# Three pairs of neighbouring RWKV stages become one stage each

## The chip, the cores and the metric

The kernel runs on one core of one Trainium2 chip. The core has a matrix engine (TensorE, called PE in the profile, with PEld for its weight loads), a vector engine (VectorE, DVE), an activation engine (ScalarE, ACT), GpSimd (POOL) and SyncE (SP), which issues most of the DMAs. The metric is the time of one execution on the device in microseconds, the median over several runs.

## The reference

One decoder block over 256 tokens plus 16 meta tokens, width 2048: a norm, one wide projection `w_in`, two token mixers in parallel, a gated merge, the output projection, and a SwiGLU feed-forward. The mixers are RWKV-7 (16 heads of 64) and FoX, a softmax attention with a forget gate (16 heads of 64). The part that this change touches is RWKV's recurrence over time,

```python
def step(S, inp):
    r_t, w_t, k_t, v_t, a_t, b_t = inp
    sa = jnp.einsum('bhvk,bhk->bhv', S, a_t)
    S = (S * w_t[:, :, None, :] + sa[..., None] * b_t[:, :, None, :]
         + v_t[..., None] * k_t[:, :, None, :])
    return S, jnp.einsum('bhvk,bhk->bhv', S, r_t)
```

followed by a group norm per head, a bonus term and a gate. Everything is float32.

## The kernel before

Weights stream from HBM in blocks of 128 x 1024. Each is split into a rounded high part and a rest (`wh` on ACT, L321; `wl` on DVE, L322), and the products high x high, high x low and low x high are summed in PSUM by the faster float32 mode of PE. L351 to L353 are these matmuls with three instructions for each weight tile (`f`, `k`, `v`, `r`), L427 and L429 the form with two (`zg`, `gt`, `up` and FoX's q). Buffers for the split weights are four deep.

RWKV and FoX are worked in four groups of four heads each. For group g the order of the weight jobs is k, v, r, the small LoRA products, FoX's q, k, v, and then two gate jobs (`zg`); for g = 3 the remaining gate jobs follow. The recurrence is cut into chunks of 64 tokens, with the meta tokens as a chunk of 16 ahead, so that most of it becomes small matmuls. All this small work of a group is a Python generator, `rwkv_bg` (from L724), which yields at the end of every stage the time after which its next stage is due; `fox_bg` is the same for FoX, and `head_norms` serves both.

The planner that interleaves them is `slot` (L383): PE's order is written out by hand, and after each pair of weight tile and k index (a slot: 340 ns of planner time for 272 columns, 322.5 for 258, 320 for 256) it looks for the stream that has been due the longest, runs one stage of it, and then lets none run until the larger of GAP = 250 ns and MIX = 0.47 times the PE time that the stage counted. Planner time is a plain sum of slots; it does not contain the stages' own time. `pe_mm` counts 4 x columns / 2.4 ns for a call, `pe_tr` 128 / 2.4 ns. A FoX stage that needs PE's aux buffers waits up to HOLD = 3500 ns for a stage of the RWKV chain, so that both run as one. Only PE's order is fixed so; the order on DVE, ACT and POOL is made by the compiler's scheduler out of the program's dependences.

A call of `pe_mm` in full float32 leaves two records in the trace, a transpose one.

The stages of `rwkv_bg` around the change, in order, each with what it needs of the aux pool (four PSUM buffers, 8 - PSM):

| stage | lines | PE work, calls | aux buffers | read out by | yields (ns) |
|---|---|---|---|---|---|
| mat, m = 0 | 790 to 798 | 8 matmuls, 64 rows, both heads of a pair side by side | 2 | DVE, 128x512 each (L796) | 2900 |
| mat, m = 1 | the same | 8 more | 2 | DVE | 2900 |
| mat0 | 799 to 829 | 4 matmuls of 80 columns for the meta chunk | 2 | DVE (L805); then DMAs L814, L816, L820 and POOL copies L823, L827 | 2300 |
| bonus (bs) | 831 to 839 | 4 matmuls against a block of ones | 2 | DVE (L837) | 1200 |
| trbk, m = 0 | 846 to 852 | 4 transposes | 1 | ACT (L850) | 1400 |
| trbk, m = 1 | the same | 4 | 1 | ACT | 1400 |
| trv | 853 to 861 | 4 transposes | 1 | ACT (L859) | 1100 |
| tr0 | 862 to 870 | 4 transposes (`tr` in the trace) | 1 | ACT (L866, L868) | 1600 |
| lane solve | 872 to 893 | none; 31 steps of two operations on DVE (L881, L883) on the table `ln` | | | 1000 after each fourth step, 24000 at its end |
| chain | 895 on | rhs, u, QT, X, s, y, ... | 1 or 2 | ACT, DVE | |

The table `ln` of the lane solve is gathered from the mat blocks NK through DRAM: NK to `d1` (L814 and L816), `d1` to `ln` (L820). Its result goes back the same way (L887, L891, L892) and is first used by the chain. The other stages that matter near these are FoX's k norms (`fk`: L644 to L648, two aux buffers, four matmuls in two pairs, each pair into one buffer), FoX's value transposes (`pvm`, `pv`: L1082 to L1088, two buffers), and the previous group's `yT` (four transposes, one buffer).

Of the kernel before, what the change touches and what calls it, by code (L numbers as in the profile page):

```python
# [62 lines left out]

HOP = 3050
PREP = 5200
LANE = 24000
GAP = 250

HOLD = 3500
# [17 lines left out]
Y_MAT = 2900  # L87
Y_NEXT = 2300
Y_BONUS = 1200
Y_TRBK = 1400  # L90
Y_TRV = 1100
Y_TR0 = 1600
Y_RHS = 1400
Y_U = 1400
Y_XT = 1400
# [7 lines left out]
def hybrid_block(ctx, tc, A, out, dbg=None):  # L103
# [18 lines left out]
    def aux_ps(name):  # L122
        return psa.tile([P, 512], F32, tag="aux", name=name)
# [251 lines left out]
    def pe_mm(out_, lhsT, rhs, start, stop, skip=False):  # L375
        clock[2] += 4 * max(lhsT.shape[-1], rhs.free_size()) / 2.4
        nc.tensor.matmul(out_, lhsT, rhs, start=start, stop=stop, skip_group_check=skip)

    def pe_tr(out_, in_, ident_):
        clock[2] += P / 2.4  # L380
        nc.tensor.transpose(out_, in_, ident_)
# [284 lines left out]
    def rwkv_jobs(g):  # L666
# [24 lines left out]
        def mul(w):  # L691
            (uh, ul), (gh, gl) = w
            gg = box["gg"] = ot(f"gg{g}")
            for m in range(2):
                ms = slice(m * P, (m + 1) * P)
                ps = main_ps(f"g{g}{m}")[:, :T]
                for k in range(2):
                    mm3(ps, gh[:, k, ms], gl[:, k, ms], sgh[:, k, :], sgl[:, k, :], k == 0, k == 1)
                nc.vector.tensor_copy(gg[:, m, :], ps)
            with tc.manual_schedule(engines={nc.scalar.engine}):  # L700
                for nm, i, dh, dl, bname in (("sig", 0, twh, twl, "w0"), ("aa", 1, adh, adl, "a0")):
                    dst = box[nm] = et(f"{nm}{g}")
                    for m in range(2):
                        ms = slice(m * P, (m + 1) * P)
                        ps = (aux_ps if i == 0 else main_ps)(f"{nm}{g}{m}")[:, :L]
                        mm3(ps, uh[:, i, ms], ul[:, i, ms], dh, dl, True, True)
                        nc.scalar.activation(dst[:, m, :], ps, AF.Sigmoid, bias=vc(bname, 2 * g + m))

                nc.scalar.preload_act_table_set("natural_log_exp_and_others")
            spawn(rwkv_bg(g, box), HOP)  # L710
# [3 lines left out]
    def hb(h):  # L714
        return slice(h * HD, (h + 1) * HD)

    def tok(c):

        return slice(0, HD) if c < 0 else slice(NMETA + c * HD, NMETA + (c + 1) * HD)

    def bcast(ap, n):
        return ap.unsqueeze(1).to_broadcast([P, n, ap.shape[1]])

    def rwkv_bg(g, box):  # L724
# [64 lines left out]
        for m in range(2):  # L789
            pss = [aux_ps(f"mat{g}{m}{h}") for h in range(2)]  # L790
            for c in range(4):
                for h in range(2):
                    pe_mm(pss[h][:, c * P:(c + 1) * P], bk[hb(h), m, c].rearrange("p x t -> p (x t)"),
                                     ar[hb(h), :, m, tok(c)], start=True, stop=True)
            for h in range(2):
                nc.vector.tensor_tensor(NK[:, h, 4 * m:4 * m + 4, :], pss[h].rearrange("p (c w) -> p c w", w=P),  # L796
                                        bcast(mup, 4), op=ALU.mult)
            yield Y_MAT
        pss = [aux_ps(f"mat0{g}{h}") for h in range(2)]
        for m in range(2):  # L800
            for h in range(2):
# [44 lines left out]
        for m in range(2):  # L846
            ps = aux_ps(f"trbk{g}{m}")
            for c in range(4):
                pe_tr(ps[:, c * P:(c + 1) * P], bkf[:, 4 * m + c, :], ident)
            nc.scalar.activation(BK[:, :, 4 * m:4 * m + 4, :].rearrange("p h c d -> p c h d"),  # L850
                                 ps.rearrange("p (c h d) -> p c h d", h=2, d=HD), AF.Copy)
            yield Y_TRBK
        ps = aux_ps(f"trv{g}")
        for m in range(2):
            for e in range(2):
# [2 lines left out]
        for cc in range(2):  # L858
            nc.scalar.activation(SV[HD:, :, cc::2, :].rearrange("p h i d -> p i h d"),  # L859
                                 ps[hb(cc), :].rearrange("p (i h d) -> p i h d", h=2, d=HD), AF.Copy)  # L860
        yield Y_TRV
        ps = aux_ps(f"tr0{g}")
        for m in range(2):
            pe_tr(ps[:, m * P:(m + 1) * P], bk0[:, m].rearrange("p x t -> p (x t)"), ident)
# [4 lines left out]
                             ps[:NMETA, 2 * P:].rearrange("p (m h d) -> p m h d", h=2, d=HD), AF.Copy)  # L869
        yield Y_TR0  # L870

# [17 lines left out]
        for h in range(2):  # L889
            for q in range(2):  # L890
                nc.sync.dma_start(X[h * HD + 32 * q:h * HD + 32 * q + 32, :, 32 * q:32 * q + 32], d2v[h, q, :32])  # L891
            nc.sync.dma_start(X0[h * HD:h * HD + 16, :, 0:32], d2[32:, :16].rearrange("(h m) r t -> h r m t", h=2)[h])  # L892
        yield LANE, ("chain", 1)

# [554 lines left out]
```

## Time and profile before

| | us |
|---|---|
| median of three runs | 1534.19 |
| lowest, highest | 1533.04, 1534.68 |
| the profiled execution's own time | 1533.9 |
| its span, first to last instruction | 1532.2 |
| PE busy | 1525.6 |
| DVE busy | 1031.3 |
| ACT busy | 778.7 |

The four groups of RWKV and FoX lie within about the first 590 us; after them come the merge and the feed-forward, which the change does not touch. Times in the timeline are microseconds from the span's start: start, duration, engine, line, operation, output <- inputs, shape, count. An `x16` row is a run of sixteen records. A row's bracket gives the idle time of the engine before it and what ended it.

### The profile page before, as it was taken

Reading aid. Unit: us, or ns where it says so; the run is one execution under the profiler, and the core shown is the slowest. Engines: PE = TensorE matmul, PEld = TensorE weight load, DVE = VectorE, ACT = ScalarE, POOL = GpSimd, SP = SyncE. Lnnn points to the kernel's source line nnn. Section 1 sums busy time; section 2 is a strip of 40 time slices with the busy share of each in tenths; the row PEclk is TensorE's granted clock in tenths of the full one; section 3 lists DMA queues with packets and bytes.
Section 4 is the critical chain, followed back from the end, with each engine's and each line's share of the span. In section 5 each row is a group of like instructions: output and inputs, shape, how many; then the busy total and the mean of one; then the engine's idle time right before and its main releaser. Section 6 shows DMA issues by size and latency. Waiting matters only on the chain.

```text
span 1532.2 us, 25930 instructions
## 1 busy us (share of the span) xinstructions
PE 1525.6 (100%) x10113; PEld 1348.9 (88%) x10113; DVE 1031.3 (67%) x1859; ACT 778.7 (51%) x1176; POOL 102.6 (7%) x182
## 2 busy tenths in 40 slices
PE   9999999999999999999999999999999999999998
PEld 9999999999989888998888888888888888888887
DVE  7888698689689768776566566656556665444443
ACT  7654665565475545554455455545445554333332
POOL 2111202302202100000000000000000000000000
PEclk9999999999999999999999999999999999999999
DMA  8667456646646757767566666666666666666663
GB/s 270 172 173 195 130 144 191 170 125 170 184 125 168 215 140 232 234 218 236 186 182 182 191 186 187 191 187 186 190 189 185 189 192 186 189 203 206 188 203 104
DMA packets 211643, 283.30 MB, mean 185 GB/s; under 512 B 24064, under 2 KB 128528, under 8 KB 211520
## 3 DMA queue, kind: packets, MB, share of 16 engines
q1 hardware_dynamic: 206912, 277.51, 61.8%
q10 hardware_dynamic: 4608, 4.13, 0.8%
q8 instruction: 79, 1.29, 0.4%
q14 instruction: 44, 0.36, 0.1%
HBM read 274.36 MB, written 7.24 MB: 184 GB/s over the span
## 4 chain that ended last, share of the span: by engine, by line
PE 99%; DMA 0%; DVE 0%; ACT 0%; SPq 0%; issue 0%; ACTq 0%
PE up L427 11%; PE gt L427 10%; PE zg L427 8%; PE dn L1312 5%; PE dn L1311 5%; PE dn L1310 5%; PE up L429 5%; PE gt L429 5%; PE zg L429 4%; PE f L351 2%; PE f L353 2%; PE f L352 2%; PE f L427 2%; PE br L351 2%; PE br L352 2%; PE br L353 2%
## 5 line engine op out<-in xcount | busy, mean ns | idle before, releaser
L322 DVE TENSOR_TENSOR wl<-raw,wh 128x1024 fp32r<-128x1024 f32 x488 | 598.8, 1228 | 414.2 <-ACT wh L321 413.7
L321 ACT ACTIVATE wh<-raw 128x1024 fp32r<-128x1024 f32 x488 | 515.9, 1058 | 605.6 <-PE dn L1311 141.5
L427 PE MATMUL gt<-hts,wh 128*128 128x512 f32 x704 | 245.0, 394 | 0.0
L427 PE MATMUL up<-hts,wh 128*128 128x512 f32 x704 | 244.9, 394 | 0.0
L429 PE MATMUL gt<-hts,wl 128*128 128x256 f32 x660 | 186.2, 282 | 0.0
L429 PE MATMUL up<-hts,wl 128*128 128x256 f32 x660 | 186.0, 282 | 0.0
L427 PE MATMUL zg<-xhl,wh 128*128 128x512 f32 x512 | 182.4, 401 | 0.0
L427 PEld LDWEIGHTS up<-hts,wh 128*128 128x128 f32 x704 | 130.1, 188 | 26.4
L427 PEld LDWEIGHTS gt<-hts,wh 128*128 128x128 f32 x704 | 130.1, 188 | 26.3
L1311 PE MATMUL dn<-wh,acl 128*128 128x512 f32 x352 | 138.7, 394 | 0.0
L1312 PE MATMUL dn<-wl,ach 128*128 128x512 f32 x352 | 138.3, 393 | 0.0
L1310 PE MATMUL dn<-wh,ach 128*128 128x512 f32 x352 | 138.1, 392 | 0.0
L429 PE MATMUL zg<-xhl,wl 128*128 128x256 f32 x480 | 135.0, 281 | 0.0
L429 PEld LDWEIGHTS up<-hts,wl 128*128 128x128 f32 x660 | 124.7, 189 | 1.8
L429 PEld LDWEIGHTS gt<-hts,wl 128*128 128x128 f32 x660 | 124.7, 189 | 1.8
L427 PEld LDWEIGHTS zg<-xhl,wh 128*128 128x128 f32 x512 | 94.3, 188 | 19.4 <-issue 0.7
L429 PEld LDWEIGHTS zg<-xhl,wl 128*128 128x128 f32 x480 | 90.6, 189 | 1.2
L1310 PEld LDWEIGHTS dn<-wh,ach 128*128 128x128 f32 x352 | 66.0, 188 | 15.7
L1311 PEld LDWEIGHTS dn<-wh,acl 128*128 128x128 f32 x352 | 66.1, 188 | 15.4
L1312 PEld LDWEIGHTS dn<-wl,ach 128*128 128x128 f32 x352 | 66.1, 188 | 14.7
L351 PE MATMUL f<-xhl,wh 128*128 128x272 f32 x256 | 76.3, 298 | 0.0
L353 PE MATMUL f<-xhl,wl 128*128 128x272 f32 x256 | 73.7, 288 | 0.0
(463 smaller groups left out, 2787.6 us busy)
## 6 DMA issues: line engine op xcount, KB each, us to landing
raw<-in_w_gate_up_dram SPq DMA_DIRECT2D x176, 512.0 KB, 4.4
raw<-in_w_in_dram SPq DMA_DIRECT2D x160, 512.0 KB, 3.9
raw<-in_w_down_dram SPq DMA_DIRECT2D x88, 512.0 KB, 4.7
raw<-in_w_o_dram SPq DMA_DIRECT2D x32, 512.0 KB, 3.9
raw<-in_w_branch_a_dram SPq DMA_DIRECT2D x16, 512.0 KB, 4.6
raw<-in_w_branch_b_dram SPq DMA_DIRECT2D x16, 512.0 KB, 3.7
zgd<-zg ACTq DMA_DIRECT2D x30, 128.0 KB, 3.8
gate<-zgd SPq DMA_DIRECT2D x15, 256.0 KB, 4.6
```

What stands on the lines that cost most here:

```text
L321: nc.scalar.activation(th, rr, AF.Copy)
L322: nc.vector.tensor_tensor(tl, rr, th.bitcast(F32), op=ALU.subtract)
L351: nc.tensor.matmul(ps, wh, ah, start=first, stop=False)
L352: nc.tensor.matmul(ps, wh, al, start=False, stop=False)
L353: nc.tensor.matmul(ps, wl, ah, start=False, stop=last)
L427: nc.tensor.matmul(ps.rearrange("p (a t) -> p a t", a=2), wh, act, start=first, stop=last)
L429: nc.tensor.matmul(ps[:, :T], wl, act[:, 0, :], start=False, stop=False)
L1310: nc.tensor.matmul(o, ah[:, kt, ts_], hi, start=first, stop=False)
L1311: nc.tensor.matmul(o, al[:, kt, ts_], hi, start=False, stop=False)
L1312: nc.tensor.matmul(o, ah[:, kt, ts_], lo_, start=False, stop=last)
```

## The change

The second mat block no longer yields, so mat0 runs in the same stage. The two trbk blocks become one stage, and trv and tr0 one. The distances that fell away are added to others: `Y_TRBK` is 2800 in place of twice 1400, `Y_TR0` 2700 in place of 1100 and 1600, and the 2900 that stood between mat and mat0 go to `LANE`, the distance between the end of the lane solve and the chain.

```diff
-LANE = 24000
+LANE = 26900
-Y_TRBK = 1400
-Y_TRV = 1100
-Y_TR0 = 1600
+Y_TRBK = 2800
+Y_TR0 = 2700
@@ rwkv_bg, mat
                 nc.vector.tensor_tensor(NK[:, h, 4 * m:4 * m + 4, :], pss[h].rearrange("p (c w) -> p c w", w=P),
                                         bcast(mup, 4), op=ALU.mult)
-            yield Y_MAT
+            if m == 0:
+                yield Y_MAT
@@ rwkv_bg, trbk
             nc.scalar.activation(BK[:, :, 4 * m:4 * m + 4, :].rearrange("p h c d -> p c h d"),
                                  ps.rearrange("p (c h d) -> p c h d", h=2, d=HD), AF.Copy)
-            yield Y_TRBK
+        yield Y_TRBK
@@ rwkv_bg, trv
             nc.scalar.activation(SV[HD:, :, cc::2, :].rearrange("p h i d -> p i h d"),
                                  ps[hb(cc), :].rearrange("p (i h d) -> p i h d", h=2, d=HD), AF.Copy)
-        yield Y_TRV
         ps = aux_ps(f"tr0{g}")
```

## The prediction

> **What bounds the kernel now.** I read the page first: span, busy shares, granted clock and the chain of work that ended last.
>
> ```profile
> span 1532.2 us, 25930 instructions
> PE   1525.6 (100%) x10113; PEld 1348.9 (88%) x10113; DVE 1031.3 (67%) x1859; ACT 778.7 (51%) x1176; POOL 102.6 (7%) x182
> PEclk9999999999999999999999999999999999999999
> PE 99%; DMA 0%; DVE 0%; ACT 0%; SPq 0%; issue 0%; ACTq 0%
> ```
>
> TensorE (PE) is busy for all but 6.6 us of the span, at full clock, and 99% of the chain is PE. So only two things can move the time: the length of the PE instruction stream, or a new moment in which PE stands still. DVE, ACT, POOL and the queues count only through such a moment. A busy PE hides short stalls, so I read start times in the timeline instead of busy time: in the stream of weight matmuls a start follows the last at a fixed pitch, and what a stage inserts is the stretch of starts less that pitch. The columns are start, duration, engine, line, operation.
>
> **The mat stages (group 2), each with the weight matmuls around it.**
>
> ```profile
> 343.98 0.29 PE L353 MATMUL f<-xhl,wl 128*128 128x272 f32 x1
> 344.20 1.16 PE L377 MATMUL mat<-ar,bk 64*128 64x128 f32 x16
> ...
> 345.52 0.29 PE L352 MATMUL f<-xhl,wh 128*128 128x272 f32 x1
> ...
> 346.52 0.29 PE L647 MATMUL fk<-nhfk,bones 128*128 128x272 f32 x1
> ...
> 346.77 0.29 PE L647 MATMUL fk<-nhfk,bones 128*128 128x272 f32 x1
> ...
> 349.13 0.29 PE L353 MATMUL f<-xhl,wl 128*128 128x272 f32 x1
> 349.35 0.46 PE L377 MATMUL mat<-ar,bk 64*80 64x16 f32 x8
> ...
> 349.98 0.29 PE L352 MATMUL f<-xhl,wh 128*128 128x272 f32 x1
> ```
>
> The two fk starts are two pitches apart: 346.77 - 346.52 = 0.25 us. From the weight matmul ahead of the second mat stage to the second one behind it, 345.52 - 343.98 = 1.54 us; less two pitches the stage costs 1.29 us. The mat0 stage costs 349.98 - 349.13 - 0.25 = 0.60 us.
>
> What of this is the price of coming and going? The trace has the same kind of small stage alone and in company:
>
> ```profile
> 330.44 0.29 PE L353 MATMUL f<-xhl,wl 128*128 128x272 f32 x1
> 330.65 0.45 PE L377 MATMUL u<-R,X 64*64 64x64 f32 x8
> 330.93 0.40 PE L377 MATMUL y<-S,ar 64*64 64x64 f32 x8
> ...
> 331.50 0.29 PE L352 MATMUL f<-xhl,wh 128*128 128x272 f32 x1
> ...
> 333.12 0.29 PE L353 MATMUL f<-xhl,wl 128*128 128x272 f32 x1
> 333.34 0.45 PE L377 MATMUL y<-sv,NK 128*64 128x64 f32 x8
> ...
> 333.95 0.29 PE L352 MATMUL f<-xhl,wh 128*128 128x272 f32 x1
> ```
>
> Sixteen records in one stage cost 331.50 - 330.44 - 0.25 = 0.81 us, eight alone 333.95 - 333.12 - 0.25 = 0.58 us. Eight more in company therefore cost 0.23, and a stage of its own costs 0.35 us for the change of form there and back. Putting mat0 behind the second mat block removes one such change. Its bounds are 0 (the change from 128 to 80 columns costs as much as the change to the weight matmuls) and 0.35 (as u and y). I take 0.30, nearer to u and y, because both blocks keep the same two 64-row halves; 0.05 is left for the odd column count. Four groups: **-1.2 us**, bounds -1.4 and 0.
>
> The rows show that a change of tile form costs PE time. The Trainium skill, TensorEngine Tiling (Array Packing), section Key Properties, says the same in general: changing the tiling mode drains the engine; by that rule too the pair mat and mat0 would save one drain and the sum stays.
>
> **The transposes.** Here the same reading gives another answer:
>
> ```profile
> 111.42 0.28 PE L429 MATMUL zg<-xhl,wl 128*128 128x256 f32 x1
> 111.54 0.60 PE L381 MATMUL trbk<-ident,bk 128*128 128x128 f32 x4
> ...
> 112.21 0.28 PE L429 MATMUL zg<-xhl,wl 128*128 128x256 f32 x1
> ...
> 237.06 0.28 PE L429 MATMUL zg<-xhl,wl 128*128 128x256 f32 x1
> 237.18 0.27 PE L381 MATMUL pvm<-ident,vv 128*16 128x128 f32 x1
> ...
> 238.07 0.28 PE L429 MATMUL zg<-xhl,wl 128*128 128x256 f32 x1
> ...
> 254.12 0.40 PE L427 MATMUL zg<-xhl,wh 128*128 128x512 f32 x1
> ...
> 254.47 0.39 PE L427 MATMUL zg<-xhl,wh 128*128 128x512 f32 x1
> ```
>
> A gate slot (one L427, one L429) is 254.47 - 254.12 = 0.35 us. Four transposes cost 112.21 - 111.42 - 0.35 = 0.44 us; the stage of six (pvm, pv) costs 238.07 - 237.06 - 0.35 = 0.66 us. Both are 0.11 us each with nothing left over: these use the whole array and pay no entry. Eight in one stage will cost 0.88 = 2 x 0.44. Merging trbk with trbk and trv with tr0 saves **0.0 us** of PE stream, bounds 0.1 either way over the eight merges (the two digits of the rows). Their PSUM copies are still four in number, two behind each merged stage, with 2700 to 2800 ns of planner time to the next.
>
> **PSUM buffers: a stall that comes.** The aux pool has four. In the code the second mat block takes two and mat0 two; merged, they hold all four at once. In groups 1 to 3 the next stage that needs any is fk (the k norms of FoX), which needs two: one per pair of its matmuls. Today it finds the first mat block's two free. After the change it must wait until DVE has read the second mat block out (NK, L796):
>
> ```profile
> 346.57 1.28 DVE L796 TENSOR_TENSOR NK<-mat,mup 128x512 f32<-128x512 f32 x2
> ...
> 102.48 1.29 DVE L796 TENSOR_TENSOR NK<-mat,mup 128x512 f32<-128x512 f32 x2 [0.76 <-PE mat L377]
> ...
> 103.98 0.29 PE L647 MATMUL fk<-nhfk,bones 128*128 128x272 f32 x1
> ```
>
> In group 2 the copies end about 347.2 and 347.85. DVE comes to them late, at 346.57, though PE wrote the blocks by 345.4. How late is fk? Before, it is at 346.52, three slots behind mat. The planner's gap after a stage is 0.47 of the stage's counted PE time: for 8 mat calls 0.47 x 8 x 4 x 128 / 2.4 = 802 ns, for the merged stage (8 x 213 + 4 x 133) x 0.47 = 1053 ns, just over three slots of 340, so fk slips one slot: +0.37 us (three pitches). With +0.30 for mat0's eight records fk comes at 346.52 + 0.67 = 347.19. Its first pair finds its buffer just free at 347.2; its second, 0.25 later at 347.44, waits until 347.85 plus the signal, some 0.45 us. In group 0 DVE is early (copies done by 103.77, fk at 103.98 + 0.3): no wait. Taking groups 1 and 3 like group 2, whose DVE work at this place is the same (the norm of the group before): **+1.4 us**. Bounds: 0 (DVE gets there half a microsecond sooner) and, if one more 1.22 us split stands ahead of the copies, 3 x (0.45 + 1.22) = 5.0.
>
> The Trainium skill, TensorEngine Tiling (Array Packing), section PSUM Bottleneck, warns of this side: tiling makes PE faster but not the emptying of PSUM. It speaks against merging tiled stages; the sum by it is that of the rows above.
>
> **PSUM buffers: a stall that goes.** The pvm/pv stage, clean at 237.18, is not so in group 2:
>
> ```profile
> 358.35 0.28 PE L429 MATMUL zg<-xhl,wl 128*128 128x256 f32 x1
> 358.47 0.27 PE L381 MATMUL pvm<-ident,vv 128*16 128x128 f32 x1
> 358.77 0.44 PE L381 MATMUL pv<-ident,vv 128*128 128x128 f32 x2
> ...
> 359.61 0.28 PE L429 MATMUL zg<-xhl,wl 128*128 128x256 f32 x1
> ...
> 358.29 0.42 DVE L837 TENSOR_TENSOR bo<-bs,v 128x256 f32<-128x256 f32 x1
> ```
>
> It costs 359.61 - 358.35 - 0.35 = 0.91 us, 0.25 over the clean one: pv starts as DVE's L837 ends, which empties the bonus stage's buffer. After the change bonus and trbk come 2900 ns of planner time earlier while pv keeps its place (its due time hangs on the v job), so L837 is long done. Group 3 has the same stages at the same distances; I take the same: **-0.5 us**, bounds -0.5 and 0.
>
> **The stages behind.** From the second mat block to the chain the distances add to 2900 + 2300 + 1200 + 1400 + 1400 + 1100 + 1600 + 7 x 1000 + 24000 = 42900 ns of planner time before, and 2300 + 1200 + 2800 + 2700 + 7000 + 26900 = 42900 after. Each stage is rounded up to the next slot of 320 to 340 ns; three fewer roundings bring the chain forward by up to three slots. It meets FoX's score stage because FoX waits up to HOLD = 3500 ns for it, and it still comes second after such a shift. A meeting lost costs one change of form, 0.35 us: I take 0, bounds -0.7 and +0.7.
>
> The lane solve (DVE, L881 and L883) moves some 3 us forward, and with it the two DMA hops that bring its table (L814, L816, then L820 on SP's queue, among the weight loads); L816 now goes out right behind L814.
>
> ```profile
> 119.12 0.19 DVE L881 TENSOR_TENSOR lt<-lx,ln 108x31 f32<-108x31 f32 x1 [1.34 <-DMA ln<-d]
> ...
> 250.61 1.22 DVE L322 TENSOR_TENSOR wl<-raw,wh 128x1024 fp32r<-128x1024 f32 x1
> ...
> 241.00:255.00 14.00, 14.00 (x81) 12.26 (x81) 13.17 (x37) 6.23 (x10) 4.03 (x7) 1.00 0.59 167
> ```
>
> In group 0 DVE stood 1.34 us for that table. Solve and table move by the same 2900 ns but for the roundings, so the wait changes by a microsecond at most. Behind it in DVE's queue stand the weight splits (L322), for which PE waits. Their cover: the split that ends at 251.83 is for the load whose first matmul is at 254.47 (counted in order, eight slots a load), 2.6 us ahead. In the stretch 241 to 255, DVE is busy 13.17 of 14.00 us (third pair of columns), so a longer wait there is not made good at once. Cost 0 while it grows by less than 2.6 us; without that cover, microsecond for microsecond.
>
> **The sum**, against the profiled execution's own 1533.9 us (1.7 beyond its span, 0.3 under the runs' median of 1534.19): -1.2 - 0.0 - 0.5 + 1.4 = -0.3, so 1533.6 for such an execution and **1533.9 us** for the median.
>
> **The rivals.**
> - *The fk wait does not come.* DVE reads the second mat block in time, as in group 0. For it: half a microsecond suffices. Against it: DVE's order at 346.57 has no cause in the parts changed. Time: 1534.2 - 1.2 - 0.5 = 1532.5.
> - *Slower: the copies of the second mat block fall behind one more weight split.* PE then stands 0.45 + 1.22 = 1.7 us at fk in each of groups 1 to 3: 1534.2 - 1.7 + 5.0 = 1537.5. It decides once the three waits together pass 1.7 us, and is measurable from 4.8 us. For it: a split follows NK in the same DVE queue, and that order is made anew when the stages move. Against it: the copies would have to be overtaken by work that follows them now.
> - *Slower: the lane solve stands for its table* until the 2.6 us of cover are gone, say 4 us in three groups: 3 x 1.4 - 0.3 = +3.9, 1538.1. Against it: today only group 0 waits.
> - *It does nothing of what it says:* PE pays the change of form between mat and mat0 too (bound 0), and neither wait changes: 1534.2.
> - *All terms go one way:* no fk wait, the full 0.35 per merged mat stage (-0.2 more), two meetings gained (-0.7), and the entries of the eight merged transpose stages cost more than the rows show (-0.1): 1531.5 for the terms with a row; 1530.8 with as much again unseen. For it only that each is possible.
>
> **How the numbers follow.** Chances: forecast 0.46, no fk wait 0.23, split ahead 0.13, lane table 0.04, nothing 0.09, all one way 0.05. Runs of this kernel span 1533.04 to 1534.68, so 0.2% (3.1 us) is about what can be told from no change. The forecast, the first rival and "nothing" lie inside it, 0.78 together; a part of the two slower rivals that stays short of 3.1 us comes in (0.03), and the lower tail of the first rival goes out (0.03): 0.78 the same. Slower: 0.17 - 0.03 = 0.14. Faster: 0.05 + 0.03 = 0.08. The forecast's own range is 1533.0 to 1535.0; the range to hold 8 in 10 reaches down past the first rival, to 1531.8, and up to most of the slower one, 1537.0.
>
> **What would show it.** Right: one mat stage of 24 records per group costing 1.6 us in place of 1.29 and 0.60; eight transposes in 0.88 us; a gap of about 0.4 us between fk's second and third matmul in groups 1 to 3 and none in group 0; pvm/pv at 0.66 in every group; rhs still in one stage with sc. Wrong: a pair cost near 1.9 for mat (the entry is not saved); no gap at fk, or one over 1 us; any PE wait for wl between the lane steps. The forecast itself falls if the median leaves 1533.0 to 1535.0.

## The result, and the profile after

The changed kernel takes 1537.3 us, the median of 16 runs (1536.55 to 1538.29), against 1534.11 (1533.04 to 1534.81) of the kernel before: a ratio of 1.0021, 95% interval 1.0014 to 1.0028. It is slower by 3.2 us. The forecast was 1533.9, with a range up to 1537.0.

The page of the profile after, in the lines that answer to those of before:

```profile
span 1535.0 us, 25943 instructions
PE   1525.0 (99%) x10113; PEld 1348.8 (88%) x10113; DVE 1031.8 (67%) x1859; ACT 777.0 (51%) x1176; POOL 100.9 (7%) x182
PE 98%; DVE 1%; ACT 1%; DMA 0%; SPq 0%; issue 0%; DVEq 0%; ACTq 0%
```

PE has the same number of instructions and 0.6 us less to do; the span is 2.8 us longer. What is new are waits of PE. The waits view, for PE, showed no wait within the four groups before. After, it has two (columns: who waited for whom, us in total, times, longest); fk's waits, under 0.4 us each, are no rows there and show only in the start times:

```profile
PE tr L380 <- ACT sv L859: 2.6, 2, 1.3
...
PE trbk L380 <- ACT bt L850: 0.9, 1, 0.9
```

Most lines of the changed kernel stand one lower than before: `tr`, `trv` and `trbk` are L380 (before L381), `wl` is L321, the weight matmuls are L350 to L352, L426 and L428.

Taking each stage as in the prediction (stretch of PE starts less the undisturbed pitch) and adding all stages up to the end of the four groups gives one figure, called stage total below: 103.51 us before, 106.85 after, +3.34. Its parts:

| | before | after | difference, four groups |
|---|---|---|---|
| second mat block and mat0 | 1.29 + 0.59 | 1.52 | -1.45 |
| eight transposes without a wait | 2 x 0.44 | 0.88 | 0.0 |
| pvm/pv, groups 2 and 3 | 0.91, 0.87 | 0.66 | -0.46 |
| fk, groups 2 and 3 | 0.50 | 1.08, 1.10 | +1.18 |
| trbk, group 1 | 2 x 0.44 | 1.96 | +1.08 |
| trv and tr0, groups 2 and 3 | 2 x 0.44 | 2.38, 2.38 | +3.00 |

They add to 3.35. PE's timeline of group 2 shows three of them (mat, fk, tr0), with one row from DVE's (NK is read out from the mat buffers):

```profile
343.39 0.29 PE L352 MATMUL f<-xhl,wl 128*128 128x272 f32 x1
343.61 1.39 PE L376 MATMUL mat<-ar,bk 64*128 64x128 f32 x24
...
345.16 0.29 PE L351 MATMUL f<-xhl,wh 128*128 128x272 f32 x1
...
346.69 0.36 PE L646 MATMUL fk<-nhfk,bones 128*128 128x272 f32 x1
...
347.28 0.37 PE L646 MATMUL fk<-nhfk,bones 128*128 128x272 f32 x1
...
355.23 0.28 PE L428 MATMUL zg<-xhl,wl 128*128 128x256 f32 x1
355.35 0.60 PE L380 MATMUL trv<-ident,v 128*128 128x128 f32 x4
357.23 0.33 PE L380 MATMUL tr<-ident,bk 128*128 128x128 f32 x1 [1.28 <-ACT sv L859]
...
357.96 0.28 PE L428 MATMUL zg<-xhl,wl 128*128 128x256 f32 x1
```

```profile
345.85 1.28 DVE L795 TENSOR_TENSOR NK<-mat,mup 128x512 f32<-128x512 f32 x2
```

The mat stage of 24 records costs 345.16 - 343.39 - 0.25 = 1.52 us. fk's two pairs are 347.28 - 346.69 = 0.59 us apart in place of 0.25: the second starts 0.15 us after DVE's second copy ends (345.85 + 1.28 = 347.13). And tr0 starts 1.9 us behind trv in the same stage, though no data runs from one to the other.

Why it waits is seen from who held the four aux buffers at 355.35. PE's, ACT's and DVE's timelines:

```profile
348.74 0.28 PE L836 MATMUL bs<-rkh,bones 128*128 128x256 f32 x1
...
354.20 0.38 PE L380 MATMUL yT<-ident,Y 128*128 128x128 f32 x2
...
355.98 1.19 ACT L859 ACTIVATE sv<-trv 64x512 f32<-64x512 f32 x2
357.51 0.38 ACT L1002 ACTIVATE ya<-yT 64x256 f32<-64x256 f32 x1 [0.34 <-DVE ya L1004]
...
357.93 0.88 DVE L1006 SCALAR_TENSOR_TENSOR ya<-ya,vcol,bo 128x256 f32<-128x256 f32 x2 [0.45 <-ACT ya L1002]
358.84 0.76 DVE L837 TENSOR_TENSOR bo<-bs,v 128x256 f32<-128x256 f32 x2
```

The bonus writes its two buffers from 348.74 on and is not read before 358.84, ten microseconds later. yT holds the third from 354.20 until its last reader, at 357.51, is done. The fourth goes to trv, and tr0 can have none until ACT has emptied that one (355.98 + 1.19 = 357.17). In group 1 the same two stages hold three buffers when trbk comes, and its second half waits for the copy of its first.

The bonus is read so late because of what L837 writes: `bo` lies in the pool tag `o`, which has three buffers for `gg` and `bo` of all groups. A new `bo` needs one that the group before still holds until its last step, which follows yT: L1006 reads the old `bo`, and L837 comes right behind it, at 358.84. In the kernel before, too, the step that reads the old `bo` (L1007 there) ends as L837 starts:

```profile
357.37 0.88 DVE L1007 SCALAR_TENSOR_TENSOR ya<-ya,vcol,bo 128x256 f32<-128x256 f32 x2 [0.45 <-ACT ya L1003]
358.29 0.76 DVE L837 TENSOR_TENSOR bo<-bs,v 128x256 f32<-128x256 f32 x2
```

But there bonus and yT were neighbours, so it cost little. The change brought the bonus 2900 ns forward and left yT where it was.

### The profile page after: what moved, and what is told of

Same layout as the page of the kernel before. It is cut to its first block, busy times and chain, and to the rows that moved or that the text cites. A ratio compares the mean times of both kernels' runs of the same rounds, so it can differ in the third digit from the quotient of the medians.

```text
span 1535.0 us, 25943 instructions
## 1 busy us (share of the span) xinstructions
PE 1525.0 (99%) x10113; PEld 1348.8 (88%) x10113; DVE 1031.8 (67%) x1859; ACT 777.0 (51%) x1176; POOL 100.9 (7%) x182
## 3 DMA queue, kind: packets, MB, share of 16 engines
q8 instruction: 79, 1.29, 0.4%
## 4 chain that ended last, share of the span: by engine, by line
PE 98%; DVE 1%; ACT 1%; DMA 0%; SPq 0%; issue 0%; DVEq 0%; ACTq 0%
PE up L426 11%; PE gt L426 10%; PE zg L426 8%; PE dn L1311 5%; PE dn L1310 5%; PE dn L1309 5%; PE up L428 5%; PE gt L428 5%; PE zg L428 4%; PE f L350 2%; PE br L350 2%; PE f L352 2%; PE br L351 2%; PE f L351 2%; PE br L352 2%; PE f L426 2%
## 5 line engine op out<-in xcount | busy, mean ns | idle before, releaser
L321 DVE TENSOR_TENSOR wl<-raw,wh 128x1024 fp32r<-128x1024 f32 x488 | 598.1, 1226 | 417.9 <-ACT wh L320 415.5
L426 PE MATMUL gt<-hts,wh 128*128 128x512 f32 x704 | 245.0, 394 | 0.0
L426 PE MATMUL up<-hts,wh 128*128 128x512 f32 x704 | 244.9, 394 | 0.0
L428 PE MATMUL gt<-hts,wl 128*128 128x256 f32 x660 | 186.2, 282 | 0.0
L428 PE MATMUL up<-hts,wl 128*128 128x256 f32 x660 | 186.0, 282 | 0.0
L426 PE MATMUL zg<-xhl,wh 128*128 128x512 f32 x512 | 180.8, 399 | 0.0
L426 PEld LDWEIGHTS up<-hts,wh 128*128 128x128 f32 x704 | 130.1, 188 | 26.4
L426 PEld LDWEIGHTS gt<-hts,wh 128*128 128x128 f32 x704 | 130.1, 188 | 26.3
L428 PE MATMUL zg<-xhl,wl 128*128 128x256 f32 x480 | 135.1, 281 | 0.0
L428 PEld LDWEIGHTS up<-hts,wl 128*128 128x128 f32 x660 | 124.7, 189 | 1.8
L428 PEld LDWEIGHTS gt<-hts,wl 128*128 128x128 f32 x660 | 124.7, 189 | 1.8
L426 PEld LDWEIGHTS zg<-xhl,wh 128*128 128x128 f32 x512 | 94.3, 188 | 19.8 <-issue 0.7
L428 PEld LDWEIGHTS zg<-xhl,wl 128*128 128x128 f32 x480 | 90.6, 189 | 1.2
L350 PE MATMUL f<-xhl,wh 128*128 128x272 f32 x256 | 76.2, 298 | 0.0
L351 PE MATMUL f<-xhl,wh 128*128 128x272 f32 x256 | 73.6, 288 | 0.0
```

The costliest lines, as they stand in the source:

```text
L321: nc.vector.tensor_tensor(tl, rr, th.bitcast(F32), op=ALU.subtract)
L350: nc.tensor.matmul(ps, wh, ah, start=first, stop=False)
L351: nc.tensor.matmul(ps, wh, al, start=False, stop=False)
L426: nc.tensor.matmul(ps.rearrange("p (a t) -> p a t", a=2), wh, act, start=first, stop=last)
L428: nc.tensor.matmul(ps[:, :T], wl, act[:, 0, :], start=False, stop=False)
```

## The experiments

Each is timed against the kernel before on the same chip; the medians of before in these sessions are 1533.93, 1533.88 and 1533.43. The ratio is not the quotient of these medians. The profiled executions differ by up to 2.6 us before the first k matmul (it starts at 29.3 to 32.0 us) and by 0 to 1.3 us in a wait at the first FoX matmul, both ahead of anything that the edits touch; the stage total leaves these out and is given beside the time. Where an expectation names a total of 108.3 or 106.4, it counts the stages of the output projection too, some 4.8 us more.

**Freeing the bonus readout.** The bonus is read into the rows of `ya` that the group owns, and yT goes to the rotating buffer.

```diff
-        bo = ot(f"bo{g}")
+        bo = ya[:, 2 * g:2 * g + 2, :]
...
-        yg = ya[:, 2 * g:2 * g + 2, :]
+        yg = ot(f"yg{g}")
...
-            nc.vector.scalar_tensor_tensor(yg[:, m, :], yg[:, m, :], vi("gn_w", m), bo[:, m, :],
+            nc.vector.scalar_tensor_tensor(bo[:, m, :], yg[:, m, :], vi("gn_w", m), bo[:, m, :],
...
-        nc.vector.tensor_tensor(yg, yg, gg, op=ALU.mult)
+        nc.vector.tensor_tensor(bo, bo, gg, op=ALU.mult)
```

> The kernel after the change, with one thing else: the bonus is read out into the rows of ya that this group owns, and the group norm's transposed output goes to the rotating o buffer instead, so the bonus readout no longer waits for the group before to free a buffer. Theory (the bonus holds two of the four PSUM buffers until the group before is through, and the merged transposes run out of buffers): the waits of PE at trbk in group 1 (1.08 us) and at tr0 in groups 2 and 3 (1.51 us each) go, the fk waits (0.58 and 0.60) stay: 1537.3 - 4.1 = 1533.2 us. Rival (a stage of two transposes blocks outruns ACT whatever else holds buffers): the 4.1 us stay, 1537.3. Rival (the loss is the mat stage): 1537.3.

Measured: 1533.21 us, ratio to before 0.9994 (0.9985 to 1.0002); stage total 102.78, 4.07 below the changed kernel. The trbk and tr0 waits are gone, the fk stages of groups 2 and 3 stay at 1.07 and 1.10 us. DVE's and PE's timelines of group 2:

```profile
348.88 0.76 DVE L837 TENSOR_TENSOR ya<-bs,v 128x256 f32<-128x256 f32 x2
```

```profile
355.05 0.60 PE L380 MATMUL trv<-ident,v 128*128 128x128 f32 x4
355.48 0.27 PE L380 MATMUL tr<-ident,bk 128*128 128x128 f32 x1
```

The bonus is read as soon as it is written, and tr0 follows trv after four transposes' time. The order and size of the stages are those of the changed kernel, so neither rival stands.

**The same move in the kernel before.**

> The kernel before the change, with the same move of the bonus readout alone. Theory: the only thing that the late readout costs there is the pv wait of 0.25 us in group 2 and 0.21 in group 3: 1534.1 - 0.46 = 1533.65 us, and pvm/pv at 0.66 us in all groups. Rival (pv waits for something else): 1534.1.

Measured: 1533.2 us, ratio 1.0000 (0.9991 to 1.0009); stage total 103.00, -0.51. pvm/pv costs 0.66 in all groups. The pv wait before was the late bonus as well; the time alone can't tell 0.5 us from nothing, the stages can.

**The mat merge alone.** Diff: `yield Y_MAT` under `if m == 0:` and LANE at 26900, on the kernel before.

> The kernel before, with mat0 merged into the second mat block and the 2900 ns put behind the lane solve, and trbk, trbk, trv, tr0 left as four stages. Theory: -1.45 (entry saved, 0.36 in each group), +1.2 (fk waits in groups 2 and 3), -0.46 (pv no longer waits), and at most 0.5 at tr0, since ACT has one stage's distance to empty each buffer: 1533.4 to 1534.0 us. Rival (the mat merge carries the loss, through the bonus that comes early): 1537.

Measured: 1534.02 us, ratio 1.0001 (0.9992 to 1.0010); stage total 103.71, +0.20. Four transposes stages with a distance each do not wait, though the bonus comes as early as in the changed kernel. fk waits in all three groups (the stage costs 1.19, 1.20 and 1.20 us in place of 0.50), one more than expected, and tr0 does not wait. The merge saves 1.45, loses 2.1 at fk and saves 0.46 at pv.

**The transposes alone.** Diff: the two trbk yields as one, trv's removed, `Y_TRBK` 2800, `Y_TR0` 2700, LANE at 24000.

> The kernel before, with only the two trbk merged and trv with tr0, LANE at 24000. The bonus stays close ahead of the group before's last step. Theory: bonus (two) and yT (one) leave one buffer when the eight trbk transposes come in groups 1 to 3, so the second four wait for ACT's copy of the first, about 1.0 us each; trv and tr0 come 2800 ns later, when the bonus has been read, and do not wait: 1534.1 + 3.0 = 1537.1 us, with no entry saved and no wait at fk. Rival (the loss comes from moving the bonus forward): 1534.1.

Measured: 1536.27 us, ratio 1.0014 (1.0005 to 1.0023); stage total 105.58, +2.07. The trbk stages of groups 1 to 3 cost 1.74 us each, 0.86 over eight free transposes; trv and tr0 do not wait, and pv is free of its wait (-0.46). PE's timeline:

```profile
354.58 0.60 PE L380 MATMUL trbk<-ident,bk 128*128 128x128 f32 x4
355.82 0.66 PE L380 MATMUL trbk<-ident,bk 128*128 128x128 f32 x4 [0.64 <-ACT ya L1001]
```

Here the second half waits for a reader of yT, not for its own first half: whichever buffer comes free first. So merging costs at both places of the bonus, and moving the bonus only changes which merged stage meets the three held buffers. The wait was a seventh smaller than expected, and the expectation had not counted the pv wait that goes.

**fk later.** Added to the changed kernel, `yield N_SUM + 700` for FoX's k norms, without and with the freed bonus.

> The kernel after the change with only FoX's k norms 700 ns later. Theory: the fk waits go (-1.2), the trbk wait of group 1 and the tr0 waits of groups 2 and 3 stay (4.1): 1537.3 - 1.2 = 1536.1 us. Rival (all waits come from the crowding that begins at fk): 1533.

Measured: 1536.67 us, ratio 1.0017 (1.0008 to 1.0025); stage total 106.15, 0.70 below the changed kernel. The stages with the trbk and tr0 waits keep their cost to 0.01 us (1.97, 2.38, 2.38 us), so these waits do not start at fk. fk is left with 0.21 and 0.23 us of wait: two slots are not quite enough.

> own_bonus with FoX's k norms put 700 ns (two slots) later, so that DVE has read the second mat block before fk asks for its buffers. Theory (fk waits only for that readout): the fk waits of 0.57 and 0.60 us go and nothing takes their place: 1533.2 - 1.2 = 1532.0 us, total of all stages 106.4 us against 108.3 before. Rival (the wait moves to the bonus stage, which then needs buffers still held by fk and mat0): 1533.2.

Measured: 1532.42 us, ratio 0.9988 (0.9979 to 0.9996); stage total 102.05. The wait did not move to the bonus (0.48 us, as free); 0.20 and 0.24 are left at fk.

> own_fk with the k norms 1400 ns later in place of 700, behind the bonus stage in place of ahead of it in group 2. Theory (what is left of the fk wait, 0.20 and 0.24 us, is the same readout of the second mat block): it goes or moves to the bonus stage, at most the same size: stage total 101.6 to 102.05 us, 1532.0 to 1532.4.

Measured: 1531.63 us, ratio 0.9987 (0.9978 to 0.9996); stage total 101.66. The rest of the fk wait is gone.

**What the transposes' merge is worth with buffers free.** The mat merge alone, with the freed bonus and fk 700 ns later.

> Only mat0 merged into the second mat block, transposes in four stages as before the change, with the bonus readout freed and the k norms 700 ns later. Theory (transposes have no entry price, so merging them is worth nothing once buffers are free): the same as own_fk, 1532.0 us, total of stages within 0.1 us of it. Rival (each stage has a price, 0.1 us or more): 0.8 us or more above own_fk in the total of the stages.

Measured: 1532.18 us, ratio 0.9988 (0.9979 to 0.9996); stage total 101.62. That is 0.43 below own_fk, and fk's remaining 0.44 there is the whole of it: here the k norms start 3.7 us behind the mat stage in group 2, against 3.3 in own_fk, and find their buffers. Against own_fk14, with no wait either and eight stages fewer, it is 0.04 apart. A transposes stage has no price of its own.

**The group before earlier.** On the changed kernel, NORM = 3000 in place of 6500.

> The kernel after the change, with NORM at 3000 ns in place of 6500, so that the last step of the group before (yT and what follows) comes 3500 ns of planner time sooner. No buffer is added and no stage is split. Theory (the bonus readout waits for that last step, and holds two PSUM buffers so long): the trbk wait of 1.08 and the two tr0 waits of 1.51 us go; yT now falls among mat, fk and bonus, where it holds one buffer more, so fk may wait up to 1 us longer in each of groups 1 to 3: 1537.3 - 4.1 + (0 to 3), 1533.2 to 1536. Rival (trv and tr0 wait for each other whatever the bonus does): the tr0 waits of 1.51 us stay.

Measured: 1540.51 us, ratio 1.0042 (1.0029 to 1.0056): well above what was expected, stage total 109.86. The tr0 waits did go: PE's timeline shows trv and tr0 without a wait in group 2, as in the others.

```profile
361.03 0.60 PE L380 MATMUL trv<-ident,v 128*128 128x128 f32 x4
361.46 0.27 PE L380 MATMUL tr<-ident,bk 128*128 128x128 f32 x1
```

Its waits view shows where the time went instead:

```profile
PE yT L380 <- DVE Y L991: 2.6, 1, 2.6
...
PE trbk L380 <- ACT ya L1002: 1.0, 1, 1.0
PE trbk L380 <- ACT bt L850: 0.9, 1, 0.9
```

In group 1 yT now comes before DVE has its input ready, and PE stands; that stage costs 2.76 us over a free one. The stages behind it cost more too, but not by waiting. The windows view of PE (stretch, its length, busy time and count, granted clock, DMA share, GB/s) and three fk starts show why:

```profile
224.00:225.00 1.00, 1.00 (x9) 0.80 0.62 217
225.00:226.00 1.00, 1.00 (x8) 0.50 0.00 0
...
230.00:231.00 1.00, 1.00 (x6) 0.50 0.59 96
231.00:232.00 1.00, 1.00 (x9) 0.79 0.38 52
232.00:233.00 1.00, 1.00 (x11) 1.00 0.00 0
```

```profile
230.59 0.43 PE L646 MATMUL fk<-nhfk,bones 128*128 128x272 f32 x1
230.81 0.43 PE L646 MATMUL fk<-nlfk,bones 128*128 128x272 f32 x1
231.04 0.43 PE L646 MATMUL fk<-nhfk,bones 128*128 128x272 f32 x1
```

From about 224.6 to 231.3 PE had half its clock. Starts there are 0.23 us apart in place of 0.125, so the mat stage costs 1.42 us more and fk 0.49, with its starts evenly spaced. An estimate from the two figures, 6.7 us at half clock, is a loss of some 3.3 us in this execution, weight matmuls included; 1.91 us of it are in the stage total. In the changed kernel, whose longest listed wait is 1.3 us, the granted clock is 1.00 through all four groups. The trace shows the order, a long wait and then the lower clock; no run here isolates what sets it off.

In groups 2 and 3 bonus and yT hold their three buffers when trbk comes, so the trbk wait that left group 1 comes up there (1.10 and 1.21 us), and fk waits 0.57 and 0.70. The late last step can't just be called for sooner.

## Why the prediction was wrong, by its own steps

- *What bounds the kernel* was right: only PE's stream and its waits move the time.
- *The mat stages* were right in kind and a little small: -1.45 us in place of -1.2. The merge saves 0.36 a group, at the upper bound given (0.35).
- *The transposes* in PE's stream were right, 0.0. The step failed in what it said of their buffers, that two copies behind each merged stage have 2700 ns to the next. It counted the pool's buffers for fk and not for the merged transposes: inside a merged stage the second half needs its buffer 0.44 us after the first, and one buffer was free. This is the term that was missing: +4.1 us, which own_bonus takes away and fk_late does not. The terms that the sum did have measure -1.45 + 0.0 - 0.46 + 1.18 = -0.73 us, in place of -0.3.
- *A stall that comes* was right in kind: 1.18 us in place of 1.4. That the two are so close is partly luck: group 1 had none, because DVE reached the copies sooner there, and groups 2 and 3 waited 0.58 and 0.60 in place of 0.45, both pairs a little. In mat_only all three groups waited, 0.70 each.
- *A stall that goes* gave the right number (-0.46) by luck, for a wrong reason: "so L837 is long done". L837 did not move with the bonus; it waits for the group before. pv was free because its place now lay behind that, not because the bonus had been read. The row quoted, pv starting as L837 ends, was half the story; that L837 itself starts behind L1007, on a buffer of `o`, was one step further back in the same view. Read there, the bonus's two buffers would have been counted as held until the group before is done, past trbk at the least.
- *The stages behind*: the chain still meets FoX's scores in one stage in every group, and no wait for a split weight appears, so the lane solve cost PE nothing.
- The slower rival gave 1537.5, near the measured 1537.3, but by another mechanism: no split came between the copies and fk. It was not right.

## What to carry to other kernels

When a stage is moved, follow what it writes as well as what it reads: a PSUM buffer is held until its reader can write, and a rotating SBUF buffer behind that reader can tie it to work that did not move. When two stages become one, count the buffers that are free at that moment, because the second half now asks for its own within half a microsecond of the first. Merge only stages for which coming and going has a price: here two blocks on half the array's rows saved 0.36 us each time, and transposes on the whole array saved nothing and lost up to 1.5 us.

## What the runs showed of the hardware that was not expected

Transposes between weight matmuls have no measurable price of entry: 0.44 us for four, 0.66 for six, 0.88 for eight, and 0.04 us over eight stages merged or not. A wait of 2.6 us on PE was followed by 6.7 us at half the clock (norm_early, group 1), which by the estimate above cost more than the wait itself (3.3 us).

The kernel could be made faster than both: with the freed bonus and fk later, 1531.63 us (ratio to before 0.9987, 0.9978 to 0.9996), and by the stage totals that gain is the four mat merges and the two pv waits, 103.51 - 101.66 = 1.85 us against 1.45 + 0.46.
